# One decoder layer for a prompt and eight samples: three query blocks projected by column, first weights tiles halved

## Chip, cores and metric

The kernel runs on one core of a Trainium2 chip. The metric is the device time of one execution in microseconds, as the median of several runs.

## What is computed

One layer of a hybrid decoder works on 256 prompt tokens and 8 sample tokens of width 1024, all in fp32. Each token goes through a modulated RMS norm and one wide projection `w_in`, whose column blocks of 512 are queries, keys, values and gates of two kinds of heads. Cut to what matters here:

```python
h = rms_norm(x, norm1_w) * (1.0 + sc1[:, None]) + sh1[:, None]
z = h @ w_in
rq, rk, rv, rg, aq, ak, av, iq, ik, iw = jnp.split(z, ...)
q = rope(rq...)                                   # retention heads
aq = rope(rms_norm(aq.reshape(B, T, 8, 64), q_norm_w), pos)
iq = rope(iq.reshape(B, T, 8, 64), pos)           # indexer: picks the keys
s = jnp.einsum('bqhd,bqkhd->bqhk', q, k_sel) * (D_HEAD ** -0.5)
p = jax.nn.softmax(s, axis=-1)
x = x + g1 * (concat([ret_out, att_out]) @ w_out)
x = x + g2 * moe_top4_of_32(norm2(x))             # 32 experts, 12.6 MB of weights each
```

`rope` multiplies by cosines and adds the other half of the head (32 of its 64 values, exchanged) times sines. The query norm divides each head of each token by its root mean square.

## The kernel before

**Two halves.** The preparation does everything up to the router; then the 32 experts follow one after the other, with all 402.7 MB of expert weights read once. Every weights load goes through `weights()` (its `load` is line 167), issued on the sync queue into a ring of tiles: in the preparation four tiles of 2 units (a unit is 128 rows of 1024 floats, 0.52 MB), and from the experts on seven tiles of 4 units (`ring2`, in the space that the preparation's tiles give free), the four of 2, and two more of 4 and 2: 42 units. An expert takes 24 units. A tile whose turn it is takes what is left of the expert, at most its size, and is loaded anew when its last reader is done.

**A row block.** `zblock(col)` (line 538) projects 512 columns with 128 tokens as the stationary side and the 512 weight columns as the moving side, twice for the 256 prompt tokens; the 32 rows with the eight samples go as small matmuls into four column strips (line 541), are copied by ScalarE (line 546) and gathered by four matmuls with `rep4` (line 548). The result has tokens on partitions. `rope` (lines 509 to 512) runs two GpSimd products on half heads, one VectorE product and one VectorE sum on each 128 tokens. `to_T` (line 570) then transposes four 128 x 128 squares on TensorE and copies them with ScalarE, since the scores need head values on partitions.

**A column block.** `zblock_t(col)` (line 558) projects with 128 weight columns as the stationary side and all 288 token columns as the moving side, so its result already has head values on partitions; before, only the retention gate (column 1536, read by ScalarE at line 1106) uses it.

**The three query blocks.** The indexer's queries (column 3584) are projected first, with loads and half-blocks interleaved with the second half of the first modulation, `ada_half(1)`; their rope stands in segment `iqr`. The attention queries (2048) go through `normed` with `head_norm` (lines 519 to 525), and the retention queries (0) stand before segment `rqr`. `acc()` gives PSUM banks from a ring of three, `trp()` and `thp()` from two each, `smp()` one. `prompt_scores` adds the mask and takes the softmax, with one ScalarE exponential for each head (line 1045), a bias on a pointer and the constant scale 0.125.

**Order.** Each engine runs its instructions in one fixed order, worked out ahead from the program's order shifted by the table `PRIO`, one number for each named segment. A `chain()` adds an order by hand.

**Experts.** `expert()` multiplies 64 gathered rows with 16 units of gate and up weights (line 1581, two records to a matmul, four records to a unit) and 8 units of down weights (line 1591). Between these, `gather_next(e)` gathers the rows for a later pair of experts, and after expert 1 `output_bias()` takes a weights tile for the output biases (lines 1640 to 1657).

Of the kernel before, what the change touches and what calls it, by code (L numbers as in the profile page):

```python
# [15 lines left out]
ALU = mybir.AluOpType  # L16
# [34 lines left out]
def _consts():  # L51
# [17 lines left out]
    c["sin"] = np.concatenate([sp[:128], sp[128:], ss], 1)  # L69
# [51 lines left out]
def hybrid_step(ctx, tc, A, L, O, KP, KT, DEC, poff, toff, dbg=None, stop=None):  # L121
# [378 lines left out]
    def rope(out, z, which, c, n, scr):  # L500

        rows = z.shape[0]
        co, si = tab[which]
        t = scr()
        u = heads(t[:rows, :64 * n], n)

# [20 lines left out]
    def zblock(col, w=None):  # L527
# [14 lines left out]
        if col == 3584:  # L542
            pe1(ins)
# [1250 lines left out]
```

## Time and profile before

| | us |
|---|---|
| median of 3 runs | 1264.1 |
| lowest and highest | 1260.33, 1264.23 |
| the profiled execution's own time | 1260.99 |
| its span, from first to last instruction | 1259.2 |
| TensorE matmuls busy | 1171.8 (93%) |
| VectorE busy | 488.6 (39%) |
| ScalarE, GpSimd busy | 134.5, 138.8 |
| moved by DMA | 475.81 MB, 378 GB/s in the mean |

All times of rows are counted from the start of the span. A matmul in fp32 leaves two records. The busy time of matmuls includes their overlap in the pipeline, so a row's duration is the time from the start of its first record to the end of its last. In the slices, 40 equal parts of the span, a digit is a busy share in tenths.

### The profile page before, as it was taken

Reading aid. Unit: us, or ns where it says so; the run is one execution under the profiler, and the core shown is the slowest. Engines: PE = TensorE matmul, PEld = TensorE weight load, DVE = VectorE, ACT = ScalarE, POOL = GpSimd, SP = SyncE. Lnnn points to the kernel's source line nnn. Section 1 sums busy time; section 2 is a strip of 40 time slices with the busy share of each in tenths; the row PEclk is TensorE's granted clock in tenths of the full one; section 3 lists DMA queues with packets and bytes.
Section 4 is the critical chain, followed back from the end, with each engine's and each line's share of the span. In section 5 each row is a group of like instructions: output and inputs, shape, how many; then the busy total and the mean of one; then the engine's idle time right before and its main releaser. Section 6 shows DMA issues by size and latency. Waiting matters only on the chain. (4 is left out here: it accounts for less than half of the span.)

```text
span 1259.2 us, 14226 instructions
## 1 busy us (share of the span) xinstructions
PE 1171.8 (93%) x5672; PEld 467.3 (37%) x5673; DVE 488.6 (39%) x1171; ACT 134.5 (11%) x289; POOL 138.8 (11%) x221
## 2 busy tenths in 40 slices
PE   7999978889999999999999898989999898998998
PEld 3443333356533334333343333333333333333332
DVE  3239865436534233332333233232323232333243
ACT  1222112211210000000000000000000000000000
POOL 3402273340010000000000000000000000000000
PEclk8999999999999999999999999999999999999999
DMA  9636896757779999999999999999999999999997
GB/s 379 269 128 237 301 367 227 233 191 305 321 292 428 427 430 428 428 430 426 430 428 430 430 426 429 431 428 428 431 428 429 430 427 431 428 429 406 427 428 313
DMA packets 53350, 475.81 MB, mean 378 GB/s; under 512 B 6896, under 2 KB 7568, under 8 KB 15520
## 3 DMA queue, kind: packets, MB, share of 16 engines
q1 hardware_dynamic: 45472, 454.04, 86.2%
q0 software_dynamic: 4432, 13.74, 3.0%
q10 hardware_dynamic: 3376, 7.09, 1.8%
q8 instruction: 46, 0.75, 0.2%
q14 instruction: 24, 0.20, 0.0%
HBM read 470.69 MB, written 4.11 MB: 377 GB/s over the span
## 5 line engine op out<-in xcount | busy, mean ns | idle before, releaser
L1581 PE MATMUL pg<-w,xg 128*64 128x512 f32 x2048 | 470.6, 600 | 35.2 <-DMA w<-lay_w_exp 33.7
L1581 PEld LDWEIGHTS pg<-w,xg 128*64 128x64 f32 x2048 | 140.7, 137 | 322.0 <-issue 267.3
L1591 PE MATMUL py<-w,sg 128*64 128x512 f32 x1024 | 236.0, 602 | 11.9 <-DMA w<-lay_w_exp 11.4
L1555 DVE TENSOR_TENSOR hb<-pt,biasT 128x512 f32<-128x512 f32 x64 | 44.3, 692 | 358.9 <-PE pt L1514 350.2
L1540 POOL TENSOR_SCALAR og<-kp,rankm,comb 128x64 f32<-128x64 f32 (+1 forms) x64 | 36.9, 593 | 848.9 <-PE pz L1525 794.6
L1591 PEld LDWEIGHTS py<-w,sg 128*64 128x64 f32 x1024 | 71.0, 138 | 146.9 <-issue 129.7
L1547 ACT ACTIVATE hs<-pg 128x512 f32<-128x512 f32 x64 | 38.2, 597 | 614.5 <-PE pg L1581 614.5
L538 PE MATMUL acc<-w,hT 128*128 128x512 f32 x208 | 102.3, 623 | 0.0
L1598 DVE TENSOR_TENSOR ys<-py,g2n 64x512 f32<-64x512 f32 x62 | 42.7, 688 | 113.3 <-PE py L1591 112.6
L1525 PE MATMUL pz<-ys,og 128*128 128x512 f32 (+1 forms) x136 | 67.8, 630 | 1.6 <-DVE ys L1594 0.8
L1528 DVE TENSOR_TENSOR x<-x,pz 128x512 f32<-128x512 f32 x68 | 46.5, 688 | 58.2 <-PE pz L1525 58.2
L1391 PE MATMUL pz<-oh,hn 128*128 128x112 f32 x480 | 58.1, 274 | 0.0
L1391 PEld LDWEIGHTS pz<-oh,hn 128*128 128x128 f32 x480 | 56.0, 192 | 0.0
L538 PEld LDWEIGHTS acc<-w,hT 128*128 128x128 f32 x208 | 37.5, 196 | 42.5 <-issue 40.6
L1560 ACT ACTIVATE sg<-hb 128x256 f32<-128x256 f32 x64 | 26.7, 416 | 224.9 <-DVE hb L1559 224.9
L1514 PEld LDWEIGHTS pt<-ident,hs 128*128 128x128 f32 x256 | 27.0, 141 | 53.2 <-issue 53.2
L1514 PE MATMUL pt<-ident,hs 128*128 128x128 f32 x256 | 42.2, 287 | 0.0
L1525 PEld LDWEIGHTS pz<-ys,og 128*128 128x128 f32 (+1 forms) x136 | 23.1, 192 | 46.0 <-issue 29.6
L1577 DVE COPY og<-pt 128x256 f32<-128x256 f32 (+1 forms) x17 | 7.2, 424 | 63.8 <-PE pt L1514 63.8
L1563 DVE TENSOR_TENSOR sg<-sg,hb 128x256 f32<-128x256 f32 x64 | 26.9, 420 | 3.9 <-DVE hb L1562 0.5
L1562 DVE SCALAR_TENSOR_TENSOR hb<-hb 128x256 f32<-128x256 f32 x64 | 27.2, 425 | 2.2
L316 PE MATMUL acc<-w,cT 128*32 128x512 f32 x128 | 24.9, 609 | 0.5 <-ACT t L848 0.5
(461 smaller groups left out, 849.5 us busy)
## 6 DMA issues: line engine op xcount, KB each, us to landing
w<-lay_w_exp SPq DMA_DIRECT2D x130, 2048.0 KB, 28.1
w<-lay_w_exp SPq DMA_DIRECT2D x122, 1024.0 KB, 26.9
w<-lay_ada_w SPq DMA_DIRECT2D x20, 1024.0 KB, 10.9
w<-lay_w_in SPq DMA_DIRECT2D x15, 1024.0 KB, 6.5
w<-lay_w_out SPq DMA_DIRECT2D x4, 1024.0 KB, 5.4
s<-qd ACTq DMA_DIRECT2D x4, 512.0 KB, 7.8
w<-lay_w_exp SPq DMA_DIRECT2D x4, 512.0 KB, 14.8
hT<-lay_x SPq DMA_DIRECT2D x1, 1152.0 KB
```

The costliest lines, as they stand in the source:

```text
L538: T.matmul(pc[c], hT[:, k, 128 * c:128 * c + 128], w[k], start=(k == 0), stop=(k == 7))
L1391: put(T.matmul(px[:, k, :n, 8:64], hn[:, c, 512 * g + 128 * k:512 * g + 128 * k + 128], oh, start=(c == 0 and k == 0), stop=(c == 1 and k ...
L1514: on_pe(T.transpose(out, in_, ident[:k, :k]))
L1525: on_pe(T.matmul(pz[n], gT[i, 128 * c:128 * c + 128], ys[i, o:o + 512], start=True, stop=True))
L1528: V.tensor_add(x[:, c, sl], x[:, c, sl], pz[n])
L1540: G.tensor_scalar(og[:, c, js], iota2[:, 0:js.stop - js.start], rank(c), gate(c), op0=ALU.is_equal, op1=ALU.mult)
L1547: S.activation(hss[h], pg[h], AF.Copy)
L1555: V.tensor_tensor(hb, pt.rearrange("p (q b t) -> p q b t", q=4, b=2), bias.rearrange("p (b h q) -> p h q b", b=2, h=2)[:, h, :, :, None].t ...
L1562: V.scalar_tensor_tensor(up, up, 1.0, gate_, op0=ALU.add, op1=ALU.mult)
L1581: on_pe(T.matmul(pg[h][64 * b:64 * b + 64, :], xg[:, k, :], w[u][:, 512 * b:512 * b + 512], start=(k == 0), stop=(k == 7)))
L1591: on_pe(T.matmul(py[64 * n:64 * n + 64, :], sgs[k // 4][:, k % 4], w[u][:, 512 * n:512 * n + 512], start=(k == 0), stop=(k == 7)))
L1598: V.tensor_mul(ys[i64, 512 * n:512 * n + 512], py[64 * n:64 * n + 64], g2n[64 * n:64 * n + 64])
```

## The change

Three blocks (columns 3584, 2048 and 0) go through a new `zcols`, which uses `zblock_t` with 264 token columns instead of 288: ScalarE copies each group of 128 columns out of PSUM, and then copies it again in four strips of 32 partitions into a second tile with the halves of each head exchanged. `rope_cols` is then one product on VectorE, one on GpSimd and one sum on VectorE over all 1024 columns. The sample columns are collected in a small tile and transposed once. For the attention queries the norm's weight is the scale of the copy, and the norm's factor is kept aside as `aqr` (squares, eight small matmuls with `hpar`, a square root with `eps64`, a reciprocal) and is used as the scale of the exponentials, in place of 0.125. The iq block's products go in two halves of k with a bank of `thp()` for the fourth group. The constants grow by 526 columns. `ring2` has nine tiles, the first four of 2 units and five of 4, instead of seven of 4. The hits for the second pair of experts stay at expert 0, and both of its gathers go to expert 1; `output_bias()` goes from expert 1 to 9. All the priorities are new.

```diff
 PRIO = {
-    "AB": -400, "AB0": -1600, "AB1": 200, "Sst": 800, "ada0_0": 100, ...
+    "AB": -400, "AB0": -1600, "AB1": 200, "Sst": 100, "ada0_0": 200, ...
...
+    c["cosT"], c["sinT"] = np.tile(cp.T, (2, 1)), np.tile(sp.T, (2, 1))
+    c["hpar"] = np.arange(14)[None, :] == 6 + (p // 64)[:, None]
...
-    def zblock_t(col):
+    def zblock_t(col, w=None, parts=1):
         seg(f"z{col}")
-        w = weights(w_block(col // 512))
-        for m in range(4):
-            p = acc()
-            for k in range(8):
-                T.matmul(p[:, :288], w[k // 2][...], hT[:, k],
-                         start=(k == 0), stop=(k == 7))
-            yield m, p
+        w = w or weights(w_block(col // 512))
+        ps_ = []
+        for k0 in range(0, 8, 8 // parts):
+            for m in range(4):
+                if k0 == 0:
+                    ps_.append(acc() if m < 3 or parts == 1 else thp())
+                for k in range(k0, k0 + 8 // parts):
+                    ins = T.matmul(ps_[m][:, :264], w[k // 2][...], hT[:, k, 0:264],
+                                   start=(k == 0), stop=(k == 7))
+                if k0 + 8 // parts == 8:
+                    if col == 3584 and m == 3:
+                        pe1(ins)
+                    yield m, ps_[m]
+
+    def zcols(col, out, other, w=None, parts=1, scale=1.0, sq=None):
+        st = t1()
+        G.memset(st, 0.0)
+        stv = st.rearrange("p (m t) -> p m t", m=4)
+        for m, p in zblock_t(col, w, parts):
+            S.activation(out[:, m], p[:, :256], AF.Copy, scale=scale)
+            if sq is not None:
+                S.activation(sq[:, m], p[:, :256], AF.Square)
+            V.tensor_copy(stv[:, m, 0:8], p[:, 256:264])
+            for a in range(4):
+                i = slice(32 * a, 32 * a + 32)
+                S.activation(other[32 * (a ^ 1):32 * (a ^ 1) + 32, m], out[i, m] if sq is not None else p[i, :256], AF.Copy)
+        sm = smp()
+        transpose(sm[:, :128], st)
+        return sm
+
+    def rope_cols(out, other):
+        bc = lambda n: C(n)[:, None, :].to_broadcast([128, 4, 256])
+        V.tensor_mul(out, out, bc("cosT"))
+        G.tensor_mul(other, other, bc("sinT"))
+        V.tensor_add(out, out, other)
...
-    pq, smq = zblock(3584, w_iq[0] + w_iq[1])
+    iqT, iqo = qkt(), t4c()
+    smq = zcols(3584, iqT, iqo, w_iq[0] + w_iq[1], 2)
...
-    aqT, aq_s = normed(2048, "q_norm_w", None, None)
+    aqT, aqo, aqq = qkt(pa_), t4c(), t4c()
+    sm = zcols(2048, aqT, aqo, scale=qwT, sq=aqq)
+    seg("n2048")
+    rope_cols(aqT, aqo)
+    aqr = pe.tile([128, 2, 8], F32, name="aqr")
+    pt = trp()
+    for c in range(2):
+        for m in range(4):
+            T.matmul(pt[:, 8 * c:8 * c + 8], aqq[:, m, 128 * c:128 * c + 128], C("hpar")[:, 6 - 2 * m:14 - 2 * m], start=(m == 0), stop=(m == 3))
+    S.activation(aqr, pt[:, :16].rearrange("p (c h) -> p c h", c=2), AF.Sqrt, bias=eps64, scale=1.0)
+    V.reciprocal(aqr, aqr)
+    aq_s = normed_rows(sm, 2048, "q_norm_w", None)
...
-        V.tensor_scalar(st[:, 0], st[:, 0], -0.125, None, op0=ALU.mult)
+        V.scalar_tensor_tensor(st[:, 0], st[:, 0], -1.0, aqr[:, c], op0=ALU.mult, op1=ALU.mult)
         for h in range(8):
-            S.activation(s[:, h, :nk], ..., AF.Exp, bias=st[:, 0, h:h + 1], scale=0.125, ...)
+            S.activation(s[:, h, :nk], ..., AF.Exp, bias=st[:, 0, h:h + 1], scale=aqr[:, c, h:h + 1], ...)
...
-    pc, sm = zblock(0)
+    rqT, rqo = s4t().rearrange("p (j t) -> p j t", j=4), t4c()
+    sm = zcols(0, rqT, rqo)
     seg('rqr')
...
+    rope_cols(rqT, rqo)
...
-    ring2 = [ctx.enter_context(pool(f"ring2_{i}")) for i in range(RING2)]
+    ring2 = [(ctx.enter_context(pool(f"ring2_{i}")), 2 if i < 4 else 4) for i in range(RING2 + 2)]
...
-    rings[:] = [(p, 4) for p in ring2] + [(ringp, 2)] * RING
+    rings[:] = ring2 + [(ringp, 2)] * RING
...
+    def between(e):
+        if e == 0:
+            nxt[0] = hits(lambda c: rankm[:, c, 2:4], 2)
+        elif e == 1:
+            gather(xgs[1], nxt[0], 0)
+        if e:
+            gather_next(e)
...
-        if e == 1:
+        if e == 9:
             output_bias()
```

## Rows read from the trace of the kernel before

**Rows 1.** The page, busy and rate by slices of 31.5 us.

```profile
DMA  9636896757779999999999999999999999999997
GB/s 379 269 128 237 301 367 227 233 191 305 321 292 428 427 430 428 428 430 426 430 428 430 430 426 429 431 428 428 431 428 429 430 427 431 428 429 406 427 428 313
```

**Rows 2.** Windows view, experts; columns are engines' busy us, PEclk, DMA share, GB/s.

```profile
372.00:1190.00 818.00, 771.73 (x3604) 290.81 (x3601) 261.75 (x534) 58.37 (x115) 31.45 (x56) 0.99 1.01 428
```

**Rows 3.** Waits of TensorE from 372 us on: total us, times, longest.

```profile
PE pg L1581 <- DMA w<-lay_w_exp: 33.7, 35, 3.1
PE py L1591 <- DMA w<-lay_w_exp: 11.4, 8, 3.1
```

**Rows 4.** Timeline of TensorE, first expert: start, us, engine, line, operation.

```profile
347.27 9.66 PE L1581 MATMUL pg<-w,xg 128*64 128x512 f32 x44 [0.68 <-POOL accs L1666]
```

**Rows 5.** Timeline of the sync queue, 349 to 372 us.

```profile
350.95 3.76 SPq L167 DMA_DIRECT2D w<-lay_w_exp  x2
358.57 0.34 SPq L1640 DMA_DIRECT2D w<-in_b_down  x1
...
362.00 9.71 SPq L167 DMA_DIRECT2D w<-lay_w_exp  x3
```

**Rows 6.** Windows view around the start of the experts.

```profile
344.00:352.00 8.00, 7.32 (x42) 4.20 (x44) 3.35 (x10) 0.00 (x0) 3.28 (x5) 1.00 0.22 80
352.00:372.00 20.00, 20.00 (x104) 8.38 (x102) 6.88 (x14) 3.31 (x5) 0.00 (x0) 1.00 0.84 327
```

**Rows 7.** Windows view, preparation: busy PE, PEld, DVE, ACT, POOL, then clock, DMA.

```profile
90.00:150.00 60.00, 56.29 (x290) 22.55 (x291) 55.44 (x204) 15.29 (x34) 11.31 (x17) 1.00 0.70 258
200.00:257.00 57.00, 48.46 (x244) 19.75 (x244) 26.44 (x55) 12.31 (x43) 14.91 (x20) 0.94 0.68 236
```

**Rows 8.** Waits of TensorE from 43 to 347 us: total us, times, longest.

```profile
PE tr L270 <- DVE t L512: 6.0, 5, 3.0
...
PE sm L548 <- ACT t L546: 2.7, 2, 1.9
```

**Rows 9.** Timeline of TensorE: a row block, then the gate block by column.

```profile
236.79 7.13 PE L538 MATMUL acc<-w,hT 128*128 128x512 f32 x16
243.85 1.06 PE L541 MATMUL sm<-w,hT 128*32 128x512 f32 x8
245.70 0.43 PE L548 MATMUL sm<-t,kp 128*32 128x128 f32 x8 [0.78 <-ACT t L546]
...
249.00 0.66 PE L270 MATMUL tr<-ident,t 128*128 128x128 f32 x4 [1.09 <-DVE t L512]
...
270.21 8.51 PE L558 MATMUL acc<-hT,w 128*128 128x288 f32 x34
```

**Rows 10.** Groups by line and form, 43 to 347 us: busy us, mean ns, idle before.

```profile
L525 DVE TENSOR_TENSOR t<-t,hr 128x512 f32<-128x512 f32 x6 | 4.1, 682 | 0.0
L1045 ACT ACTIVATE t<-t,st 128x256 f32<-128x256 f32 x8 | 3.9, 494 | 24.5 <-DVE st L1043 24.5
L509 POOL TENSOR_TENSOR t<-t,kt 128x256 f32<-128x256 f32 x4 | 3.9, 970 | 23.0 <-ACT t L1090 18.1 <-ACT t L617 5.0
...
L1048 DVE TENSOR_TENSOR t<-t,st 128x1024 f32<-128x1024 f32 x2 | 2.4, 1220 | 0.0
...
L972 PE MATMUL th<-kt,s 128*128 128x4 f32 x16 | 2.1, 244 | 0.9 <-DVE s L969 0.9
...
L1106 ACT ACTIVATE t<-acc 128x288 f32<-128x288 f32 x4 | 1.6, 410 | 18.0 <-PE acc L558 18.0
```

**Rows 11.** Windows view of two short stretches, clock and DMA share at the end.

```profile
30.00:40.00 10.00, 9.45 (x62) 2.91 (x61) 0.42 (x1) 0.00 (x0) 0.00 (x0) 1.00 1.03 411
222.00:227.00 5.00, 5.00 (x11) 2.11 (x12) 0.27 (x2) 0.00 (x0) 3.64 (x4) 0.66 0.85 297
```

**Rows 12.** DMA issues on the page: number, KB each, median us to landing.

```profile
w<-lay_w_exp SPq DMA_DIRECT2D x130, 2048.0 KB, 28.1
w<-lay_w_exp SPq DMA_DIRECT2D x122, 1024.0 KB, 26.9
```

More of the change, by code (lines that the diff above doesn't have):

```diff
@@ L195, in hybrid_step @@
     V.memset(epsc, EPS)
+    eps64 = per.tile([128, 1], F32, name="eps64")
+    V.memset(eps64, 64 * EPS)
     ones_b = per.tile([128, 128], BF16, name="ones_b")
@@ L285, in hybrid_step @@
         T.matmul(idle.rearrange("p (n m) -> p n m", n=4), ones_b, ones_b[:, None, :].to_broadcast([128, 4, 128]), start=True, stop=True)
-    sw_ = pe.tile([128, 204], F32, name="sw_")
+    sw_ = pe.tile([128, 205], F32, name="sw_")
     S.dma_start(sw_, L["small"])
@@ L488, in hybrid_step @@
     for n, w in enumerate(("q_norm_w", "k_norm_w", "idx_k_norm_w")):
-        tc_, ts_ = pe.tile([128, 3, 64], F32, name="tc", bufs=4), pe.tile([128, 3, 64], F32, name="ts", bufs=4)
-        bc = lambda ap, k: ap[:, None, :].to_broadcast([128, 3, k])
-        G.tensor_mul(tc_, cosv, bc(nw[:, n], 64))
-        G.tensor_mul(ts_[:, :, 0:32], sinv[:, :, 0:32], bc(nw[:, n, 32:64], 32))
-        G.tensor_mul(ts_[:, :, 32:64], sinv[:, :, 32:64], bc(nw[:, n, 0:32], 32))
+        c0, k = (2, "1") if n == 0 else (0, "")
+        tc_, ts_ = [pe.tile([128, 3 - c0, 64], F32, name=t + k, bufs=1 if c0 else 3) for t in ("tc", "ts")]
+        bc = lambda ap, k: ap[:, None, :].to_broadcast([128, 3 - c0, k])
+        G.tensor_mul(tc_, cosv[:, c0:], bc(nw[:, n], 64))
+        G.tensor_mul(ts_[:, :, 0:32], sinv[:, c0:, 0:32], bc(nw[:, n, 32:64], 32))
+        G.tensor_mul(ts_[:, :, 32:64], sinv[:, c0:, 32:64], bc(nw[:, n, 0:32], 32))
         tab[w] = (tc_, ts_)
-    tc_, ts_ = pe.tile([128, 3, 64], F32, name="tc", bufs=4), pe.tile([128, 3, 64], F32, name="ts", bufs=4)
+    tc_, ts_ = pe.tile([128, 3, 64], F32, name="tc", bufs=3), pe.tile([128, 3, 64], F32, name="ts", bufs=3)
     G.tensor_scalar(tc_, cosv, 0.125, None, op0=ALU.mult)
@@ L503, in rope @@
         co, si = tab[which]
+        c = 0 if which == "q_norm_w" else c
         t = scr()
@@ L540, in zblock @@
                 g = 32 * (k % 4)
-                ins = T.matmul(sm[g:g + 32, :], hT[:, k, 256:288], w[k], start=(k < 4), stop=(k >= 4))
-        if col == 3584:
-            pe1(ins)
+                T.matmul(sm[g:g + 32, :], hT[:, k, 256:288], w[k], start=(k < 4), stop=(k >= 4))
         t = t2()
@@ L613, in hybrid_step @@
     seg("iqr")
-    iqT = qkt()
-    for c in range(2):
-        z, o = t2(), t2()
-        S.activation(z, pq[c], AF.Copy)
-        rope(heads(o, 8), heads(z, 8), "one", c, 8, t2)
-        to_T(iqT[:, :, 128 * c:128 * c + 128], o)
+    rope_cols(iqT, iqo)
     seg("iqs")
@@ L791, in hybrid_step, with normed_rows @@
     G.memset(mixT[:, :, 256:288], 0.0)
+    def normed_rows(sm, col, w, outs):
+        seg(f"ns{col}")
+        z = t1()
+        S.activation(z, sm[:, :128], AF.Copy)
+        head_norm(heads(z, 2), 2, t1)
+        o = pe.tile([128, 128], F32, name=w + "s")
+        rope(heads(o, 2), heads(z, 2), w, 2, 2, t1)
+        if outs is not None:
+            sample_rows(outs, o)
+        return o
     def normed(col, w, outp, outs):
@@ L804, in normed @@
             to_T(tt[:, :, 128 * c:128 * c + 128], o)
-        seg(f"ns{col}")
-        z = t1()
-        S.activation(z, sm[:, :128], AF.Copy)
-        head_norm(heads(z, 2), 2, t1)
-        o = pe.tile([128, 128], F32, name=w + "s")
-        rope(heads(o, 2), heads(z, 2), w, 2, 2, t1)
-        if outs is not None:
-            sample_rows(outs, o)
-        return tt, o
+        return tt, normed_rows(sm, col, w, outs)
     def sample_rows(n, o):
@@ L1084, in hybrid_step @@
         V.tensor_copy(modT[:, i].rearrange("p (j q) -> p j q", j=2), pt[:, :256].rearrange("p (q j r) -> p j q r", q=4, j=2)[:, :, :, 0])
-    pc, sm = zblock(0)
+    rqT, rqo = s4t().rearrange("p (j t) -> p j t", j=4), t4c()
+    sm = zcols(0, rqT, rqo)
     seg('rqr')
-    rqT = s4t().rearrange("p (j t) -> p j t", j=4)
-    for c in range(2):
-        z, o = t2(), t2()
-        S.activation(z, pc[c], AF.Copy)
-        rope(heads(o, 8), heads(z, 8), "one", c, 8, t2)
-        to_T(rqT[:, :, 128 * c:128 * c + 128], o)
+    rope_cols(rqT, rqo)
     z = t1()
@@ L1697, in hybrid_step @@
         scatter = expert(w, xgs[e // 2 % 2][:, :, e % 2], biasT[:, :, e], lambda c: rankm[:, c, e:e + 1],
-                         lambda c: comb[:, c, e:e + 1], gs[:, e:e + 1], scatter or nothing, lambda: gather_next(e), pr_, 0 if solo else e % 2, solo or e % 2 == 1, e == NE - 1)
-        if e == 1:
+                         lambda c: comb[:, c, e:e + 1], gs[:, e:e + 1], scatter or nothing, lambda: between(e), pr_, 0 if solo else e % 2, solo or e % 2 == 1, e == NE - 1)
+        if e == 9:
             output_bias()
@@ L1754, in build @@
     lay["small"] = np.concatenate([f32("norm1_w").reshape(8, 128).T] + [f32(n)[None].repeat(128, 0) for n in ("q_norm_w", "k_norm_w", "idx_k_norm_w")]
[L1755 removed]
+                                  + [f32("ret_gn_w").reshape(4, 128).T, np.tile(f32("q_norm_w"), 2)[:, None]], 1)
     pt = np.asarray(inputs["page_table"], np.int32)
```

14 lines of the change are left out of this document (8 added, 6 removed), and 24 rows, old and new, of the table PRIO.

## The prediction

> **What bounds the kernel now.** I read the slices of the page first [rows 1]. The DMA row is at 9 or more from the thirteenth slice on, about 378 us into the span, and stands below that before; the rate row settles at 426 to 431 GB/s there. So the run has two halves: a preparation that does not fill the DMA engines, and the 32 experts, which do. A window over most of the second half confirms it: DMA share 1.01 at 428 GB/s, while TensorE is busy 771.73 of 818 us [rows 2]. TensorE's waits in that half are for expert weights, 33.7 and 11.4 us, and hardly for anything else [rows 3]. The end of the run is therefore the start of the experts plus the bytes still to come at 428 GB/s, plus whatever time the DMA engines stand idle after the start. Only two things can shorten it: an earlier start, or less idle DMA around the start.
>
> The idle DMA can be read directly. The first expert's matmuls begin at 347.27 [rows 4]. By then all weight tiles are full, so the queue waits for the first one to be read: the next load goes out at 350.95, after 16 matmul records (a 4-unit tile holds weights for 16). At 358.57 the next tile of the ring goes to the output bias, and the next weights follow only at 362.00 [rows 5]. The windows give the loss: shares of 0.22 over 8 us and 0.84 over the next 20 make 6.2 + 3.2 = 9.4 us without transfers [rows 6].
>
> What sets the start is the preparation, and there TensorE is nearly full: 56.29 of 60 us in one stretch, 48.46 of 57 in another [rows 7]; in the first, VectorE is full too (55.44). TensorE's waits in the preparation are short and scattered; the two kinds that belong to row-form projections are 6.0 us for VectorE's rope sums ahead of transposes, and 2.7 us for ScalarE's copy of the sample rows [rows 8].
>
> **The change, part by part.** *TensorE, one projected block.* By rows, 16 records take 7.13 us, the last of them 0.59 of it by itself, so 6.54/15 = 0.436 us each; 32 are 13.95. The sample rows take 16 records, 1.0 us for each eight: 2.0. The re-gathering by rep4 is 0.4, and eight transposes at 0.11 (four in 0.66, the last of them 0.33) are 0.9 [rows 9]. Sum 17.2 us. By columns the same product is 64 records of 264 columns. The gate block runs 288 columns that way: 34 records in 8.51 us, 0.245 each [rows 9]; 264 columns should take 0.225. 64 make 14.4, one transpose 0.1: 14.5 us. So 2.7 us saved per block.
> - Block 0 (rq): 2.7 us.
> - Block 2048 (aq): the norm needs eight products against hpar, 16 records; the nearest row, 16 records with four columns, took 2.1 us [rows 10]. Saved: 0.6.
> - Block 3584 (iq): its first half hides today in the wait for the second half of the first modulation. 24 records of this work fit there: 16 x 0.436 + 1.0 = 8.0 us. By columns the third group needs an accumulator bank that ada_half(1) holds until that wait ends, so at most three of four groups' first halves fit, 24 x 0.225 = 5.4. The 2.6 us that move out eat the saving. I take 0; bounds 0 and 2.7.
> - Gate block 1536: 64 records shorter by 0.020: 1.3 us.
>
> *Waits around the blocks.* Block 0 has a wait of 0.78 us before rep4 and one of 1.09 before its transposes [rows 9]; both steps go. I count 1.0 of 1.9, because a wait for another VectorE tile lies between them and becomes what is late next. Bounds: 0, and all 8.7 us of both kinds.
>
> *ScalarE.* Each block issues 4 x 5 = 20 activations of 256 columns (aq also four squares) where there were five of 512. The nearest row is 0.410 us for 288 columns [rows 10]; 20 make 8.2 us. A group's five make 2.05 us while TensorE works 3.6 us on the next group, so they are covered as long as ScalarE has no other long work in its queue. I take 0 for the end; the cover gone is a rival below. The exponentials get a second pointer. The rows put 0.494 us for 256 columns with a bias pointer against 0.410 for 288 without [rows 10], so between 0 and 0.09 us for one more, 16 times: at most 1.4 us, off TensorE; I take 0. The Trainium skill, "ScalarE: Activation LUTs", section "What ACT_TABLE_LOAD costs", gives 93 ns for such an operand; no run here shows it yet.
>
> *VectorE and GpSimd.* The rope was four VectorE operations of 512 columns and four GpSimd ones of 256; now two of 1024 and one of 1024. VectorE: 4 x 0.682 (the row of a product of that form) against 2 x 1.220 [rows 10], the four small copies eat the rest: equal. GpSimd: the same columns, at most 4 x 0.970 either way [rows 10]: equal. For aq VectorE also drops two reductions and two products of 512 columns, 4 x 0.682 = 2.7 us by the row of a product, in the stretch where it is full; I count nothing for it but see it as the reason why no new wait forms there. The zeroing of st by GpSimd lies before the block and is covered by it.
>
> *Constants.* cosT, sinT and hpar add 526 columns of 128 rows, 0.27 MB, in a stretch that is DMA-bound at 411 GB/s [rows 11]: 0.6 us later tables, charged in full.
>
> *Start of the experts.* The first tile now holds two units, so it is free after 8 records, not 16: the first reload is 1.85 us sooner (half of 350.95 - 347.27). After that TensorE frees 1.05 MB every 1.7 us and the queue needs 2.45 us for it, so the 3.2 us of gaps behind it should close, the more so as the bias no longer takes a tile there and a lap's tiles add up to whole experts (8 + 16, then 18 + 6 units). Sum 5.0 of 9.4 us; bounds 1.85 and 9.4. The bias at expert 9 and the gather moved from expert 0 to 1 issue the same instructions and the same two transfers later, where the transfers and not TensorE set the end: 0. The four small tiles cost more issues on the sync queue (an issue takes 0.34 us [rows 5], its transfer 2.45): covered.
>
> *The new order* of the priorities moves work that I cannot price; it is what the own range of the forecast holds.
>
> **Sum.** Start: 0 + 0.6 + 2.7 + 1.3 + 1.0 - 0.6 = 5.0 us earlier. After it: 5.0 us less idle DMA. The profiled execution took 1261.0 us, a span of 1259.2 and 1.8 around it; 10.0 less is 1251.0. It lies 3.1 below the median of the runs shown, 1264.1, so the median forecast is **1254.1**, rounded to 1254.
>
> **Rivals** (all as medians).
> - *Start unchanged*: VectorE's and GpSimd's chains set the start, not TensorE. For it: VectorE at 55.44 of 60 us [rows 7]. Against: TensorE is as full, and 2.7 us of VectorE work goes from there. Only the 5.0 us after the start count: 1259. The mirror, that the smaller tiles do nothing and only the start moves, gives the same.
> - *Waits go too*: the new order also removes the 8.7 us of both kinds of waits instead of 1.0: 7.7 less, 1246.
> - *Small loads are slow*: per lap of 42 units two loads of 2 MB become four of 1 MB; 402.7 MB are 18.3 laps, so 73 loads more of 1.05 MB, 77 MB. The stretch at 411 GB/s [rows 11] is full of loads of 1 MB and less; at that rate 77 MB cost 7.4 us more than at 428: 1261.5. Against: the 428 GB/s of the experts already hold 122 loads of 1 MB beside 130 of 2 MB [rows 12]. The Trainium skill, "DMA: Bandwidth & Descriptors", section "Measured (HBM→SBUF, 128 partitions, SWDGE, issued from GpSimd)", speaks for it: it lists 341 GB/s at 1 MB and 425 at 16 MB. By those figures the 77 MB would cost an estimated 46 us; the mixture of both sizes at 428 GB/s does not bear that out.
> - *ScalarE late* (the other side): its queue is in order. If other work stands ahead of a group's copies, the three accumulator banks stay held and TensorE stops. Price at one block: a run of eight exponentials, 8 x 0.494 = 4.0 us [rows 10], and the lower clock of 1.2 GHz after a pause (222 to 227, behind an idle stretch, was granted 0.66 in the mean, so 1.7 us of 5 are lost) [rows 11]: 5.6 us. One block leaves a gain, two end level with before (1265), three lose: 1271. For it: 60 more activations; against: ScalarE is busy 12.31 of 57 us [rows 7].
>
> **How the numbers follow.** Forecast 0.50 (own range 1249 to 1259, for the bounds above), start unchanged 0.17, waits go too 0.13, small loads 0.07, ScalarE late 0.13. The range leaves out the last and the edge of others: 1244 to 1264. About 0.3%, 3.8 us, can be told from no change: faster means below 1260.3, slower above 1267.9. Faster: 0.48 + 0.10 + 0.13 + 0.02 = 0.73. Same: 0.02 + 0.06 + 0.05 + 0.02 = 0.15. Slower: the rest of ScalarE late and of the edges, 0.12.
>
> **What would show it.** The first expert matmul near 342 us; records of 264 columns at 0.22 to 0.23 us each; the first reload within 2 us of that matmul and shares near 1 from 4 us after it; 428 GB/s as before in the experts. Wrong would be: an experts' rate below 425, a first expert matmul at 347 or later, or new waits of TensorE for ScalarE's copies in blocks 3584, 2048 or 0.

## The result, and the profile after

The changed kernel is slower: 1297.55 us in the median (1294.8 to 1299.29, 4 runs) against 1264.16 for the kernel before in the same job, a ratio of 1.0265 [1.0239, 1.0291]. The forecast was 1254.0 with a range to 1264. The profiled execution has a span of 1295.9 us.

The slices of the page, after; the first row is TensorE's clock, and the other two answer to [rows 1]:

```profile
PEclk8899999877999999999899999999999999999999
DMA  9725696665689999999999999999999999998997
GB/s 382 297 92 198 255 366 239 179 245 199 269 345 427 423 420 425 426 421 424 395 420 425 425 424 425 423 425 423 423 425 423 420 427 424 421 418 354 424 420 299
```

Three things are to be seen: from the thirteenth slice on the rate lies mostly at 420 to 427 and no longer at 426 to 431, there are two dips (395, where the output bias now is, and 354, where the kernel before has 406), and the clock is lower in the slices before the experts. The timeline of TensorE gives the start of the experts, the place of [rows 4]:

```profile
370.67 4.91 PE L1630 MATMUL pg<-w,xg 128*64 128x512 f32 x21 [0.30 <-DVE xg L1451]
```

So the experts start 23.4 us later (370.7 against 347.3), and the rest, from there to the end of the span, is 13.3 us longer (925.2 against 911.9). Here are windows of the kernel before, and then of the changed one. Columns: window, its length, busy PE, PEld, DVE, ACT and POOL with their instructions, TensorE's granted clock, DMA share, GB/s.

```profile
0.00:347.00 347.00, 311.81 (x1678) 145.32 (x1679) 192.18 (x571) 68.31 (x160) 101.76 (x157) 0.97 0.71 268
700.00:1100.00 400.00, 365.22 (x1689) 135.23 (x1686) 121.39 (x249) 27.96 (x55) 15.68 (x28) 0.99 1.01 429
1120.00:1140.00 20.00, 18.82 (x90) 7.62 (x86) 8.91 (x18) 1.43 (x3) 0.00 (x0) 1.00 0.95 397
```

```profile
0.00:370.00 370.00, 321.61 (x1696) 176.45 (x1698) 190.64 (x570) 85.14 (x206) 98.69 (x150) 0.90 0.68 252
305.00:329.00 24.00, 23.91 (x88) 16.14 (x89) 8.64 (x21) 3.04 (x5) 0.30 (x1) 0.57 0.57 230
368.00:376.00 8.00, 7.70 (x47) 4.32 (x47) 3.62 (x12) 0.00 (x0) 3.12 (x5) 1.00 0.56 213
376.00:384.00 8.00, 8.00 (x42) 2.97 (x39) 2.04 (x5) 2.30 (x3) 0.00 (x0) 1.00 0.99 371
600.00:700.00 100.00, 97.70 (x436) 35.58 (x432) 36.35 (x71) 6.08 (x12) 2.24 (x4) 0.97 1.01 414
700.00:1100.00 400.00, 362.00 (x1677) 135.79 (x1678) 119.05 (x245) 27.36 (x54) 15.70 (x28) 0.98 1.01 424
1160.00:1180.00 20.00, 17.70 (x79) 7.06 (x77) 8.28 (x16) 1.01 (x2) 2.33 (x4) 1.00 0.76 305
```

Up to the experts TensorE is idle for 48.4 us (370 - 321.61) instead of 35.2, and busy for 9.8 us more, at a mean clock of 0.90 instead of 0.97. The row of 305 to 329 us is the worst stretch: TensorE busy all the time, clock 0.57 in the mean, so mostly at 1.2 instead of 2.4 GHz. The waits of TensorE show one that was not there before, and ScalarE's timeline (ACTq is its queue) shows how it came about:

```profile
PE acc L569 <- ACT t L589: 11.6, 1, 11.6
```

```profile
240.28 3.64 ACTq L1066 DMA_DIRECT2D s<-vd  x4
243.96 1.56 ACTq L1289 DMA_DIRECT2D rw__2374<-lay_router_w  x1
245.56 2.14 ACTq L1292 DMA_DIRECT2D rb<-in_router_b  x1
254.45 0.94 ACT L583 ACTIVATE s<-acc 128x256 f32<-128x256 f32 x3 [18.88 <-DVE s L1076]
```

In block 0 the copies stand behind six DMA issues, which are out at 247.7, and then wait until 254.45 for a tile that VectorE's state update (line 1076) still holds. The three banks stay held, and TensorE stops for 11.6 us.

### The profile page after: what moved, and what is told of

It reads as the page before. It is cut to its first block, busy times and chain, and to the rows that moved or that the text cites. A ratio compares the mean times of both kernels' runs of the same rounds, so it can differ in the third digit from the quotient of the medians.

```text
span 1295.9 us, 14369 instructions
## 1 busy us (share of the span) xinstructions
PE 1185.4 (91%) x5691; PEld 500.0 (39%) x5692; DVE 487.9 (38%) x1173; ACT 151.3 (12%) x335; POOL 136.0 (10%) x215
## 5 line engine op out<-in xcount | busy, mean ns | idle before, releaser
L1630 PE MATMUL pg<-w,xg 128*64 128x512 f32 x2048 | 475.4, 606 | 45.7 <-DMA w<-lay_w_exp 44.8
L569 PE MATMUL acc<-hT,w 128*128 128x264 f32 x216 | 55.5, 407 | 11.9 <-ACT t L589 11.6
L547 PE MATMUL acc<-w,hT 128*128 128x512 f32 x128 | 62.5, 626 | 0.7 <-DMA w<-lay_w_in 0.7
L569 PEld LDWEIGHTS acc<-hT,w 128*128 128x128 f32 x216 | 41.8, 200 | 22.3 <-ACT t L589 12.0
L547 PEld LDWEIGHTS acc<-w,hT 128*128 128x128 f32 x128 | 23.4, 197 | 29.2 <-issue 28.1
L322 PE MATMUL acc<-w,cT 128*32 128x512 f32 x128 | 30.2, 649 | 3.4 <-issue 3.4
```

The costliest lines, as they stand in the source:

```text
L547: T.matmul(pc[c], hT[:, k, 128 * c:128 * c + 128], w[k], start=(k == 0), stop=(k == 7))
L569: ins = T.matmul(ps_[m][:, :264], w[k // 2][:, 512 * (k % 2) + 128 * m:512 * (k % 2) + 128 * m + 128], hT[:, k, 0:264], start=(k == 0), st ...
L1630: on_pe(T.matmul(pg[h][64 * b:64 * b + 64, :], xg[:, k, :], w[u][:, 512 * b:512 * b + 512], start=(k == 0), stop=(k == 7)))
```

## The experiments

Each run's time stands beside that of the kernel before in the same job. "Start" is the first expert matmul of the profiled execution, "rest" what is left of its span from there. Executions of one kernel scatter by some 5 us to either side, so a start of one profile is good to a few us, and the medians decide. The profiled execution of the kernel before took 1261.0 us, 3 to 5 below the medians of that kernel; those of runs 11 and 12 lie 6.0 below and 4.2 above theirs.

| run | kernel | median us | ratio to before | start | rest |
|---|---|---|---|---|---|
| 1 | after, block 0's copies in a tile of their own | 1294.3 | 1.0233 [1.0206, 1.0261] | 369.0 | 924.5 |
| 2 | after, old ring | 1295.93 | 1.025 [1.0223, 1.0278] | 369.0 | 923.4 |
| 3 | before, new ring | 1270.81 | 1.0036 [1.0017, 1.0055] | 348.7 | 915.8 |
| 4 | after, both of 1 and 2 | 1289.86 | 1.0207 [1.0172, 1.0242] | 366.1 | 922.1 |
| 5 | after, old order | 1281.11 | 1.0129 [1.009, 1.0169] | 353.2 | 925.8 |
| 6 | before, new order | 1288.31 | 1.017 [1.0117, 1.0223] | 375.9 | 913.1 |
| 7 | after, 64 bytes for eps64 | 1295.87 | 1.024 [1.02, 1.0281] | 371.8 | 923.2 |
| 8 | before, tiles 32 bytes further on | 1270.94 | 1.0045 [1.0025, 1.0065] | 348.7 | 919.6 |
| 9 | column blocks alone | 1267.11 | 1.0012 [0.9986, 1.0038] | 353.1 | 911.9 |
| 10 | before, ring tiles on multiples of 256 | 1260.24 | 0.9964 [0.9943, 0.9985] | 345.3 | 910.5 |
| 11 | after, eps64 in epsc's tile | 1289.76 | 1.0183 [1.0146, 1.0221] | 365.6 | 916.4 |
| 12 | 11, retention in the old order | 1275.51 | 1.0087 [1.0057, 1.0118] | 362.3 | 915.7 |
| 13 | 11, 20 wide products added | 1287.88 | 1.0176 [1.0131, 1.0222] | 369.8 | 916.5 |
| 14 | 10, one tile split in two | 1269.3 | 1.0036 [1.0014, 1.0059] | 352.0 | 915.3 |
| 15 | 9, block 0's copies in a tile of their own | 1266.09 | 1.0017 [0.9998, 1.0036] | 350.2 | 910.9 |
| 16 | 10, gate block with 264 columns | 1264.09 | 0.9987 [0.9969, 1.0005] | 352.2 | 910.4 |

**The wait in block 0, and the ring (runs 1 to 4).** The first theory was that the 11.6 us wait sets the start and that the 1 MB loads lower the rate.

```diff
-    sm = zcols(0, rqT, rqo)
+    rqe = t4c()
+    sm = zcols(0, rqe, rqo)
-    rope_cols(rqT, rqo)
+    rope_cols(rqT, rqo, rqe)
```

> Changed kernel; block 0's copies out of PSUM go to a tile of the four-buffer pool, and the rope writes the old tile. Theory (the copies wait for the tile that the state update still reads): TensorE's 11.6 us wait in block 0 shrinks to 4 us or less, the expert start comes 8 to 14 us earlier than 370.7, time 1283 to 1290. Rival (ScalarE's queue is late there anyway, or the time is lost to the new order): the wait stays above 8 us and the time within 4 us of 1297.

```diff
-    ring2 = [(ctx.enter_context(pool(f"ring2_{i}")), 2 if i < 4 else 4) for i in range(RING2 + 2)]
+    ring2 = [(ctx.enter_context(pool(f"ring2_{i}")), 4) for i in range(RING2)]
```

> Changed kernel with the ring of before (seven tiles of 4 units). Theory (more loads of 1 MB lower the stream's rate): the experts' rate returns from 419 to 424 to about 428 GB/s, some 10 us; the first reload comes 2 us later and gaps of 3 us return; time 1287 to 1292. Rival (the rate is lower for another reason, such as the address or the chip's state): rate stays at 424 or less, time 1296 to 1302.

Run 3 is the opposite edit in the kernel before, run 4 the edits of 1 and 2 together.

> Kernel of before with only the new ring (four tiles of 2, five of 4). Theory (1 MB loads slow, 1.2%): rate 423 to 425, start of the experts unchanged at 347, 10 us lost and 2 to 5 won: 1267 to 1273. Rival (my prediction's term: the ring only shortens the stall at the start): rate 428, 1258 to 1262.

> Changed kernel with both edits, own tile and old ring. Theory: the two gains add up, 1273 to 1281. Rival (they overlap, since an earlier start only finds the transfers later): within 3 us of the better of the two alone.

Both halves of the theory fell. In run 1 the wait is gone, in run 2 it is 3.0 us, and in both the start moves by 1.7 us only. Run 4 is 4.4 us below the better of the two, which is more than its rival said and far from its theory; the intervals overlap. With the old ring the rate stays at 425 GB/s from 700 to 1100 us (runs 2 and 4), and the new ring leaves the kernel before at 428 (run 3). The rows of runs 2 and 3:

```profile
700.00:1100.00 400.00, 361.22 (x1694) 135.42 (x1692) 120.21 (x248) 28.38 (x56) 13.44 (x24) 1.00 1.01 425
```

```profile
700.00:1100.00 400.00, 366.76 (x1681) 136.84 (x1682) 121.33 (x249) 27.96 (x55) 15.68 (x28) 0.98 1.01 428
```

What the new ring costs in the kernel before, 4.6 us in the ratio, lies for the most part elsewhere. One place is a branch late in the experts; windows of run 3, of run 14 (below) and of run 2:

```profile
1140.00:1160.00 20.00, 16.19 (x72) 5.79 (x73) 3.95 (x9) 1.01 (x2) 2.33 (x4) 1.00 0.84 342
```

```profile
1140.00:1160.00 20.00, 16.92 (x68) 5.95 (x68) 7.34 (x14) 1.01 (x2) 2.33 (x4) 1.00 0.78 316
```

```profile
1160.00:1180.00 20.00, 17.43 (x72) 6.30 (x70) 6.21 (x12) 0.60 (x1) 2.33 (x4) 1.00 0.70 285
```

This is the branch ahead of expert 28 (`spill`), where the loads behind it are issued late: in the changed kernel the last load ahead of it lands at 1172.7 us and the next one is issued at 1173.2. The kernel before loses 1.2 us there (20 x (1.01 - 0.95)); run 3 loses 3.4 in this window and 1.4 in the one before it, and run 14 4.6; the changed kernel loses 5.0 (20 x (1.01 - 0.76)). But run 2, the changed kernel with the old ring, loses 6.2, and run 9 (below), with the old ring and the bias at expert 1, 1.2 again. So in the changed kernel the new ring alone does not explain this gap; which tile of the ring the branch meets, which the bias at expert 9 shifts as well, is a likely cause that was not tried by itself.

Another part is TensorE's clock. Of run 3's ten executions four took 1264.9 to 1266.2 us at a mean granted clock of 0.977 to 0.982, and six 1270.8 to 1272.1 at 0.967 to 0.975.

**The order (runs 5 and 6).** The tables of priorities are exchanged, and nothing else.

> The changed kernel with the old table of priorities; everything else as changed. Theory A (the new order is wrong for this kernel: it puts ScalarE and VectorE work in front of what TensorE needs and leaves the engine at the lower clock): the first expert matmul comes back to about 350 us (370.7 in the changed kernel), stretches of TensorE's lower clock ahead of it shrink towards the 24 us of the kernel before, time about 1277 us. Rival B (the column blocks themselves cost the time, whatever the order): the first expert matmul stays at 368 us or later, time 1294 to 1300. Either way the experts' rate stays at 423 to 425 GB/s, since the order has nothing to do with it.

> The kernel before with the new table of priorities; nothing else changed. Theory A (the order alone costs the start): first expert matmul 360 us or later, about 1278 us. Rival B (the column blocks cost it): first expert matmul within 5 us of 347.3, about 1261 to 1269 us. The order was presumably made for the changed kernel, so a loss here alone does not settle A; together with the run of the changed kernel with the old order it does. Experts' rate 428 to 429 GB/s either way.

Theory A held: the new table costs 17 us in the changed kernel (1.0265 less 1.0129 of 1264) and, in the kernel before, 21 us (1.017). But not by waits. Windows of run 5, then of run 6:

```profile
0.00:353.00 353.00, 304.66 (x1697) 166.21 (x1698) 188.96 (x573) 85.11 (x206) 102.22 (x151) 0.94 0.71 265
293.00:306.00 13.00, 10.54 (x135) 8.65 (x134) 8.73 (x21) 1.91 (x5) 1.32 (x2) 1.00 0.93 373
```

```profile
0.00:375.00 375.00, 339.67 (x1674) 160.87 (x1676) 193.09 (x567) 68.80 (x160) 102.35 (x156) 0.90 0.67 248
306.00:329.00 23.00, 22.04 (x135) 16.49 (x132) 9.12 (x22) 2.54 (x4) 1.30 (x2) 0.66 0.58 235
```

TensorE is idle for 48.3 us with the old table and 48.4 with the new in the changed kernel, and for 35.2 and 35.3 in the kernel before. The same matmuls take 17 and 28 us longer, at a mean clock of 0.90 with the new table against 0.94 and 0.97. The second row of each is the same work, the retention's products: 13 us at clock 1.00, 23 us at 0.66.

Not all of the 17 and 28 us is the clock. If TensorE's busy time at the lower clock is counted half (an estimate from the clock records of the traces), the clock makes 12 of the 17 us and 21 of the 28; the rest is work that takes longer at an equal clock, for which the retention below shows one reason. All executions agree on the direction: their mean granted clock has a median of 0.960 in the changed kernel and 0.967 in run 5, 0.979 in the kernel before and 0.969 in run 6.

**The place of the tiles (runs 8, 7 and 11).** `eps64`, one float for each partition, takes 32 bytes of SBUF in the pool that lies ahead of the experts' tiles. The seven tiles of the old ring start at 50944 in the kernel before, a multiple of 256; with `eps64` the same space starts at 50976. Run 8 adds `eps64` to the kernel before, where nothing reads it; run 7 gives it 64 bytes in the changed kernel; run 11 puts it into a tile that is there:

```diff
-    epsc = per.tile([128, 1], F32, name="epsc")
-    eps64 = per.tile([128, 1], F32, name="eps64")
+    epss = per.tile([128, 2], F32, name="epsc")
+    epsc, eps64 = epss[:, 0:1], epss[:, 1:2]
```

> The kernel before with a tile of one float for each partition (eps64) that nothing reads, in the same place as the changed kernel has it, so that every tile behind it lies 32 bytes further on: the expert tiles start at 50976 instead of 50944. Nothing else is changed. Theory (tiles off a multiple of 64 bytes are written more slowly): experts' rate falls from 429 to 423 or 424 GB/s, time from the first expert matmul to the end rises by 10 to 13 us, the preparation possibly by some us too, time 1275 to 1282 us. Rival (alignment does not matter): 1262 to 1268 us, 428 to 429 GB/s.

> The changed kernel with one small tile (eps64, one float for each partition) given 64 bytes instead of the 32 it takes now. In the changed kernel this tile moves every tile behind it in SBUF by 32 bytes: the expert tiles start at 50976, no multiple of 64, where the kernel before had 50944, a multiple of 64; here they start at 51008, a multiple of 64 again. Theory (a weight tile that does not start on a multiple of 64 bytes is written more slowly): the experts' rate returns from 423 to 428 or 429 GB/s, the time from the first expert matmul to the end falls from 925 to about 913 us, time about 1285 us. Rival (the rate has another cause: more column work, the place of the arrays in HBM, output bias at expert 9): rate stays at 422 to 425, time 1295 to 1300.

> The changed kernel with eps64 in the second float of epsc's tile: nothing behind it is moved, the expert tiles start at 50944 as in the kernel before, a multiple of 256; in the run with 64 bytes for eps64 they started at 51008, a multiple of 64 and not of 128, and the rate stayed at 424. Theory (the multiple of 256 decides): rate back from 423 to 426 to 428 GB/s (what the kernel before gave with the new ring), time from the first expert matmul to the end 915 to 919 us instead of 925, time 1287 to 1292 us. Rival (something else in the changed kernel lowers the rate): 422 to 424 GB/s, 1294 to 1300 us.

The same window of the experts in runs 8, 7 and 11:

```profile
700.00:1100.00 400.00, 363.68 (x1680) 135.50 (x1678) 120.01 (x246) 26.95 (x53) 15.68 (x28) 0.99 1.01 425
```

```profile
700.00:1100.00 400.00, 367.60 (x1698) 136.89 (x1696) 120.20 (x246) 27.97 (x55) 15.70 (x28) 0.98 1.01 424
```

```profile
700.00:1100.00 400.00, 372.93 (x1738) 140.21 (x1736) 125.13 (x257) 28.38 (x56) 14.14 (x26) 0.98 1.01 428
```

At 50976 the rate falls from 429 to 425 in the kernel before, with nothing else changed, and at 50944 it is back at 428 in the changed one. In time the step is smaller than expected for the kernel before (7.7 us more from the first expert matmul to the end, 5.7 in the ratio). At 51008 (run 7), a multiple of 64 but not of 128, the rate stays at 424: the theory of 64 bytes was wrong.

Run 11 did what the theory of 256 forecast, but 50944 is a multiple of 128 too, and run 10 (below) speaks for 128. It moves the four small tiles from 4224, a multiple of 128 and not of 256, to 4352, a multiple of 256, and the rate stays at 429:

```profile
700.00:1100.00 400.00, 366.14 (x1706) 137.56 (x1708) 123.45 (x255) 28.38 (x56) 15.68 (x28) 1.00 1.01 429
```

The DMA packets in the traces, assigned to tiles by the order of the ring, say the same: a packet of 8 KB into one of the four small tiles takes 309 ns in the median at 4224 and at 4352. Into the last tile of the ring it takes 312 ns in the kernel before, where that tile lies 64 bytes off a multiple of 128, and 309 after the move; into the tiles of `ring2` 309 at 50944 and 313 at 50976.

The Trainium skill, "DMA: Bandwidth & Descriptors", section "How a descriptor splits into AXI transactions", names 256 bytes as the boundary, for the bytes that a descriptor reads: a piece that does not start on a multiple of it takes one transaction more, which begins at the boundary below. By the page's beats of 32 bytes the price of a start 32 bytes off is an estimated 0.2% (513 for 512 in 16 KB) to 0.4% (257 for 256 in 8 KB). Here the start that moves is that of the bytes written, the tiles at 4224 show no price, and the others cost more than the page's count (4 of 429, 0.9%).

**The columns alone (runs 9 and 15).** Run 9 keeps of the change only the column blocks, with the old table, the old ring, bias and gathers in their old places and `eps64` as in run 11. Run 15 adds the edit of run 1 and moves the ring's two right tiles to multiples of 256.

> Only the column blocks of the change: old table of priorities, old ring of seven tiles of four units, output bias and gathers where they were, and eps64 in the second float of epsc's tile, so that the expert tiles start at 50944 again, a multiple of 256. What the three column blocks and the shorter gate block do to the start by themselves is left. Theory A (the columns by themselves save little and open waits for ScalarE's copies and GpSimd's sums, as the run with the old order had them with 48.6 us of idle TensorE): first expert matmul at 349 to 355 us, experts' rate 428 or 429 GB/s, time 1266 to 1273 us. Rival (the columns are a gain, and the run with the old order lost it to the tiles' shift and the new ring): first expert matmul at 340 to 346 us, time 1256 to 1263 us.

> The column blocks alone (as in the run that gave 1267.1 us), with block 0's copies written into a tile of their own instead of the tile that VectorE's state update still holds, and the two tiles on the right moved to multiples of 256. Theory (the wait for ScalarE's copies in block 0 eats the saving): the wait of 6.9 us is gone, first expert matmul at 344 to 348 us instead of 353.1, time 1258 to 1263 us. Rival (another wait takes its place, as in the changed kernel, where taking this wait away moved the start by 1.7 us only): first expert matmul at 350 to 354 us, time 1263 to 1268 us.

No gain, in both (1.0012 and 1.0017). Run 9's window up to the experts and its longest waits of TensorE, then the longest of run 15:

```profile
0.00:353.00 353.00, 305.98 (x1697) 166.62 (x1698) 189.51 (x573) 85.19 (x206) 100.97 (x151) 0.93 0.71 265
```

```profile
PE acc L569 <- ACT t L589: 6.9, 1, 6.9
PE tr L276 <- DVE t L1100: 6.4, 2, 6.2
```

```profile
PE tr L276 <- DVE t L1100: 6.3, 2, 6.1
PE tr L276 <- DVE t L521: 5.7, 3, 4.7
...
PE acc L878 <- ACT t L589: 3.3, 1, 3.3
```

TensorE's work did shrink, by 5.8 us (305.98 against 311.81), at a clock that is even lower. Its idle time grew by 11.8 us (47.0 against 35.2). Other profiles bear this out: up to the first expert matmul TensorE is idle for 31 to 36 us in the kernel before and in runs 3, 8, 10 and 14, which prepare in the same way, and for 44 to 49 in the column runs 5, 9 and 15. Taking block 0's wait away leaves 3.3 us for the same copies at the next user of the rope's result (line 878), and the 6 us for VectorE behind the softmax stay: the rival, another wait in its place.

**The clock in the retention (runs 12 and 13).** With the new table the eight products of keys with queries of the second half (line 879) and the seven of scores with values of the first (line 1200) come in turns, mostly of one product each. Run 12 sets seven priorities of run 11 back, after which these come in runs of eight and seven again; on TensorE little else changes. Run 13 leaves run 11's table and adds products that nothing reads:

```diff
+    def warm(p, n):
+        for d in range(n):
+            T.matmul(p[:, :264], ident, hT[:, d, 0:264], start=True, stop=True)
...
         pS = acc()
+        warm(pS, 4)
...
         po = acc()
+        warm(po, 4)
...
             pb = [acc(), acc()]
+            warm(pb[0], 4)
```

> The changed kernel with eps64 in epsc's tile, and the old priorities for seven names alone (in1, ro0, ro1, ro2, Sst, dec, z1536). On TensorE the only difference is in the retention: eight products of keys with queries, seven of scores with values, eight of the gate, eight of scores with values and eight of queries with the state come in five runs again, where the new order takes them in turns of one or two. Theory (these turns are what the clock falls for, and with them the start): no stretch of 20 us at 1.2 GHz at 300 to 330 us, the products from the first of them to the output projection take 8 to 11 us instead of 18.6, first expert matmul at 352 to 357 us instead of 365.5, time 1276 to 1281 us. Rival (the clock falls anyway, for the idle stretches before, and the order of these products does not matter): first expert matmul at 363 to 367 us, time 1286 to 1291 us.

> The changed kernel with eps64 in epsc's tile, and 20 products of 264 columns more (ident by hT, 0.22 us each at 2.4 GHz, 4.4 us together), written into the retention's banks before they are used; nothing reads them. They lie just before the stretch in which the clock falls and in it. If the clock falls for the narrow products (64 and 128 columns on half of the rows) and the wide ones hold it up, the 20.5 us at 1.2 GHz shrink to 10 or less, and the first expert matmul comes at 358 to 366 us although there is more work; time 1281 to 1290 us. If they do not, the work comes on top at the lower clock: first expert matmul at 370 to 375 us, time 1294 to 1299 us.

The retention's stretch, from the end of the gate block to the output projection, in runs 11, 12 and 13:

```profile
295.00:319.00 24.00, 23.23 (x147) 16.95 (x146) 8.92 (x22) 2.56 (x4) 1.32 (x2) 0.66 0.56 225
```

```profile
304.00:318.00 14.00, 12.71 (x150) 9.72 (x149) 9.32 (x22) 2.79 (x5) 1.33 (x2) 1.00 0.89 362
256.00:291.00 35.00, 23.07 (x101) 13.95 (x101) 16.86 (x24) 12.61 (x35) 10.89 (x17) 0.57 0.65 228
```

```profile
301.00:325.00 24.00, 24.00 (x180) 18.33 (x179) 9.30 (x21) 2.55 (x4) 1.32 (x2) 0.93 0.23 68
```

Rows of TensorE's timeline, first of run 11, at full clock and then at the lower one, then of run 12:

```profile
301.14 0.43 PE L1200 MATMUL acc<-rows,t 128*128 128x64 f32 x2
301.51 0.48 PE L879 MATMUL acc<-s,qkT 64*128 64x128 f32 x2
301.92 0.43 PE L1200 MATMUL acc<-rows,t 128*128 128x64 f32 x2
...
303.75 0.79 PE L879 MATMUL acc<-s,qkT 64*128 64x128 f32 x2
304.47 0.69 PE L1200 MATMUL acc<-rows,t 128*128 128x64 f32 x2
305.09 0.79 PE L879 MATMUL acc<-s,qkT 64*128 64x128 f32 x2
```

```profile
309.76 1.49 PE L879 MATMUL acc<-s,qkT 64*128 64x128 f32 x16
311.18 1.77 PE L1200 MATMUL acc<-rows,t 128*128 128x64 f32 x14
```

Run 12's stretch takes 14 us at full clock instead of 24 at 0.66, and the time falls by 12 us (1.0183 to 1.0087), a little more than expected. The mean granted clock of its executions has a median of 0.966, against 0.956 in run 11. Its profile has the start at 362.3, later than expected, since this execution has another long stretch at 0.57, from 256 to 291 us behind waits. Run 13's stretch takes 24 us again, with 40 records more that were busy for 11.7 us: the added products (more than twice the 4.4 us that I had put down, as each leaves two records) cost nothing there, at a clock of 0.93 instead of 0.66. The total, 1.0176 against 1.0183, is the same; its start, 369.8, is later than the theory said. Run 13 is not clean, since the added products also left fewer of the turns. So most of this stretch's length is the clock, and the order of the narrow products, 64 and 128 columns wide, is what it fell for here: from the end of the gate block to the first turn runs 11 and 12 do the same work, with the same gap of 0.78 us, and only run 11's clock falls. A smaller part is the turns themselves: one of each kind takes 0.78 us from start to start at full clock and 1.34 at the lower one, where run 12's runs come to 0.44 a pair (1.49/8 + 1.77/7).

**A version a little faster than both (runs 10, 14 and 16).** Run 10 is the kernel before with tiles moved and nothing else:

```diff
+    ctx.enter_context(pool("al")).tile([128, 32], F32, name="al")
     ringp = ctx.enter_context(pool("ring", RING))
...
+    per.tile([128, 32], F32, name="al2")
...
-    mp.tile([128, 176], F32, name="pad")
+    mp.tile([128, 192], F32, name="pad")
```

> The kernel before with every tile of the rings on a multiple of 256 bytes: the four small tiles move from 4224 to 4352, the seven of four units from 50944 to 51200, the two on the right from 189248 and 181056 to 189184 and 180992. In the kernel before, 28 of a lap's 42 units (one unit is 4096 bytes a partition) lie on a multiple of 256 and 14 do not. Theory (a tile off a multiple of 256 is written more slowly, about 425 GB/s against more): the rate rises from 429 to 431 or 432 GB/s, time from the first expert matmul to the end falls from 912 to about 907 us, time 1258 to 1261 us. Rival 1 (a multiple of 64 was enough, all of the old tiles have it, and the run with 64 bytes for eps64 was slow for another cause): 429 GB/s and 1262 to 1268 us. Rival 2 (the tiles on different offsets help each other): rate falls, over 1268 us.

> The kernel before with all tiles of the rings on multiples of 256 bytes (1260.2 us, 0.9964), and the first tile of four units split into two of two units. This is the part of the new ring that lets the first reload start after 8 products instead of 16, with 18 more loads of 1 MB instead of about 73. Expected if the earlier reload is a gain and the price of the new ring came from its many small loads: 1256 to 1259 us, DMA share around the first expert matmul like that of the changed kernel's (3.6 us lost instead of 9.4). Rival (any change of the ring's phase makes the gap at the branch before expert 28 longer, 3.6 to 5 us lost there instead of 1.1): 1260 to 1264 us.

> The kernel before with the rings' tiles on multiples of 256 (1260.2 us, 0.9964) and the gate block's 32 products with 264 instead of 288 columns, as the changed kernel has them; nothing else. 64 records shorter by 0.020 us are 1.3 us on TensorE. If they reach the start: first expert matmul 1 to 2 us earlier, time 1257 to 1261 us. If the gate block lies beside VectorE's chain, or a different pattern of work changes the granted clock: within 2 us of 1260, not to be told apart; a loss of more than 3 us would say that a small edit moves the clock by more than it saves.

Run 10 beats both kernels, by 0.36% [0.15, 0.57] against the one before. Not for the reason given: its rate is 429 as before, and 2.0 us of the gain lie in the start and 1.4 in the rest, which one profile each cannot explain further. Run 16 has the same moves and cannot be told from the kernel before, so the gain is not confirmed.

Split tiles lose it again, and more than the rival's 1260 to 1264 (run 14). Some 3.5 us go with the gap at the branch, as that rival said. Its start is also 6.7 us later, with no edit there. The windows up to the start, run 10 and then run 14, show that TensorE is idle for as long (30.6 and 31.5 us) and busy for 6 us more, at a lower clock:

```profile
0.00:345.00 345.00, 314.43 (x1678) 145.95 (x1679) 191.77 (x571) 68.40 (x160) 101.99 (x157) 0.95 0.71 270
```

```profile
0.00:352.00 352.00, 320.48 (x1679) 147.98 (x1681) 192.69 (x571) 68.61 (x160) 102.14 (x158) 0.93 0.70 265
```

The executions agree (a median granted clock of 0.973 against 0.983 in run 10). Why the clock is lower there is open.

Run 16 shortens TensorE's work by an estimated 1.3 us and comes out 3.9 us above run 10, with a wait of 6.9 us for the copy of a block's sample rows that run 10 does not have; the intervals overlap, so the loss is not certain, but no gain is seen.

## Why the prediction was wrong

- **TensorE's saving: right, if anything too small.** 58 records of 264 columns took 13.17 us in the changed kernel, 0.227 each (0.225 forecast). In run 9 TensorE's work is 5.8 us shorter, and 14 us if busy time at the lower clock is counted half (an estimate). The terms for the work were 2.7 + 0.6 + 2.7 + 1.3 = 7.3, of which the iq block's 2.7 were not counted for the start.
- **"Waits around the blocks ... I count 1.0 of 1.9": the first step that failed.** Instead of 1.0 us less idle time there are 11.8 us more (run 9). The bounds were 0 and a gain of 8.7; I set no bound for a loss here, though each column block puts 20 copies, a VectorE sum of 1024 columns and a GpSimd product in one piece between the projection and its first reader, where the row form had two halves of tokens that overlapped. Which of these costs what was not tried, except for block 0's copies.
- **"The new order ... it is what the own range of the forecast holds": the step that cost most.** I gave it 5 us to either side. It costs 17 us in the changed kernel, half of the loss, some two thirds of it by the clock: [rows 11] had shown 0.66 in a stretch, and I priced that at 1.7 us, as something that follows a pause. Here the clock was at 0.57 for 24 us in which TensorE was busy.
- **"428 GB/s as before": the third.** The rate is 424, and the rival's small loads have little part in it (428 in runs 3 and 11, with the new ring). `eps64` has no term at all in my sum, although its 32 bytes move every tile behind it. Runs 8 and 11 put 7.7 and 8.8 us of the 13.3 on it by their profiles, and 5.7 and 10.4 by the ratios.
- **Less idle DMA at the start: right, by its mechanism.** The first reload comes at 372.6, 2.0 us after the first matmul. Shares of 0.56 and 0.99 leave 3.6 us lost (8 x 0.44 + 8 x 0.01), against 9.4 [rows 6]: 5.8 us gained, 5.0 forecast.
- **What gives it back.** The gap at the branch is 3.8 us longer (5.0 against 1.2), which I had not looked at. The bias at expert 9 costs 2.4 us (100 x 10 / 424) by the window of 600 to 700 us, where I had put 0: the transfers set the end there, so every slow one counts. No run has the bias or the gathers moved by themselves. With the place of the tiles, and less the 5.8 gained, these make 8.1 to 9.2 of the 13.3 us. Some 2 us more go with run 3's 428 instead of 429 over 900 us (an estimate); the last 2 to 3 I cannot assign.
- **ScalarE late: right in effect, wrong in cause and price.** The banks are held and TensorE stops at one of the three blocks, block 0, for 11.6 us instead of 5.6. But it was not other work in ScalarE's queue that came last: the queue stood still from 247.7 to 254.45 us for the tile that VectorE held. Taking the wait away gave 1.7 us of start, because others were right behind.
- **Exponentials.** With the second pointer the 256-column form took 0.589 us against 0.494 [rows 10], 0.095 more, just over my upper bound of 0.09. The Trainium skill, "ScalarE: Activation LUTs", section "What ACT_TABLE_LOAD costs", with its 93 ns, agrees.

By single edits the loss adds up as 1.5 us for the columns (run 9), 4.6 for the ring (run 3), 5.7 for the 32 bytes (run 8) and 17 for the order (run 5), 29 of 33.5. This is a tally and no decomposition, since the same edits weigh differently in the other kernel: the ring 1.9 us (run 2), the 32 bytes 10.4 (run 11), the order 21 (run 6).

## What to carry to other kernels

A new small tile ahead of large DMA targets is a change of its own: look where the large tiles start afterwards (here 32 and 64 bytes off a multiple of 128 cost about 0.9% of the rate). A shorter program on the bounding engine is worth what is left after its idle time and its clock: compare, up to the same point, busy time, idle time and granted clock, before believing in a wait that looks long. And a long wait is worth only its distance to the next one, which the removal itself shows.

## What the runs showed of the hardware

Weights streamed at 428 to 429 GB/s into tiles starting at 50944 and at 424 to 425 into the same tiles at 50976 or 51008; moving other tiles of the ring from a multiple of 128 to one of 256 left the rate at 429. TensorE was granted 0.66 in the mean over 24 us in which it was busy for 23.2, mostly with narrow products in turns. In runs of seven and eight the same products were granted 1.00. With wide ones put between the clock was 0.93, and 11.7 us of added work left the stretch at 24 us.
